# Weight sums with other signs, a part of them added by transfers, in a Strassen-Winograd gate/up projection

## The chip, the cores and the metric

The kernel runs on one core of one Trainium2 chip. The metric is the device time of one launch in microseconds (us). Engines are called PE (TensorE; PEld is its weight load), DVE (VectorE), ACT (ScalarE), POOL (GpSimd) and SP (SyncE, which here issues transfers only).

## The reference

One decoder layer over 512 tokens of width 2048, all in float32: a combined input projection, gated linear attention and dilated attention side by side, an output projection, and a SwiGLU feed-forward part with 5632 hidden columns. The change is in the last line.

```python
h = rms_norm(x, norm1_g)
proj = h @ w_in                     # (512, 2048) @ (2048, 6160)
...                                 # gla_mixer and dilated_mixer
x = x + mix @ w_out                 # (512, 2048) @ (2048, 2048)
h2 = rms_norm(x, norm2_g)
x = x + (silu(h2 @ w_gate) * (h2 @ w_up)) @ w_down      # w_gate, w_up: (2048, 5632)
```

## The kernel before

Every large product is computed in "pairs": 512 tokens by two times 512 weight columns (for the gate pairs 512 columns of w_gate and the same 512 of w_up), as one level of Strassen-Winograd: seven products of quarter blocks instead of eight. The eleven gate pairs (j = 0 to 10) follow the output projection, and six pairs of the down projection follow them.

**Left factors.** The class Operand holds, for each of four row groups of 2 x 256 rows, the four plain or summed quarters of the normalised activations: A11, A12, A22 and S1 to S4. Each one is kept as a high part, rounded to float32r by ACT, and a remainder made by DVE (`split`, L174 and L175). All eleven gate pairs share one operand, `opn`. It is built while the output projection ends and gate pair 0 begins (`operand_jobs`, `early_jobs`, `late_jobs`).

**Right factors.** A pair has four weight quarters per group, a and c from the first matrix, b and d from the second, each a tile of 128 x 1024 float32 (512 KB) from a pool of 12 (`load_quarter`, L222, issued by SP). The products come in the order P1, P5, P6, P3, P7, P2, P4. P1, P3 and P2 use a, d and c as they are. P5 uses b - a, P6 uses d - (b - a), P7 uses d - b and P4 uses c less what P6 used; DVE makes these sums in place (`source`, L256), one of 1024 columns for each of four products and four groups, so 16 in a pair.

**An item** is one product of one group. ACT rounds its weight tile to a high part (`wh`, L331), DVE makes the remainder (`wl`, L335), and PE does eight matmuls with the high part and four with the remainder (L361). Both `wh` and `wl` have two buffers. A pair has 28 items. `stream` runs through the items of all pairs: before the matmuls of item k it writes down the cast of k + 1, the sum of k + 2 and the remainder of k + 1.

**Results.** P1, P5 and P6 leave PSUM as `seeds` (ACT, L282), times the row scale; the later products are added by `close` (DVE, L298). For a gate pair `final_ffn` multiplies silu(gate) with up, transposes on PE (L1109), stores the product to memory (p_d, L1124), and a `sums_job` reads it back (r, L1173) and makes the down projection's left sums on DVE (L1457, L1459, L1462, L1464).

**Order.** Only the first pair has an order written out by hand. After it the framework's scheduler places the instructions of each engine by priority and by when it expects operands, so a sum can be done well before the item that needs it. Each engine then runs its list in order: an instruction that waits holds up all behind it. A load from SP waits until a tile of the pool is free.

POOL issues no transfer. It computes the reciprocal roots of the row norms, the last of them `rs2`, the row scale of the gate pairs (`output_scales`, L1396 to L1401).

Of the kernel before, what the change touches and what calls it, by code (L numbers as in the profile page):

```python
# [18 lines left out]
P = 128  # L19
# [11 lines left out]

PRODUCTS = ("P1", "P5", "P6", "P3", "P7", "P2", "P4")
UPPER_FIRST = ("P1", "P2", "P5", "P6", "P3", "P7", "P4")
SINGLE = {"P1": "a", "P3": "d", "P2": "c"}
SUMS_OF = {"P5": "ba", "P6": "da", "P7": "db", "P4": "ca"}
CLOSES = {"P3": (0, 1), "P7": (1, 1), "P2": (0, 0), "P4": (1, 0)}
# [71 lines left out]
def block_kernel(ctx: ExitStack, tc: tile.TileContext, ins, out):  # L108
# [56 lines left out]
    class Operand:  # L165


        def __init__(self, groups):
            self.groups = groups
            self.t = {}  # L170

        def split(self, name, g, src):
            a = apool.tile([P, 2, 2, 256], F32R, name=nm("A" + name), tag="A")
# [6 lines left out]
        def build(self, g, r11, r21, r12, r22):  # L180

            get = lambda r: r() if callable(r) else r
            tt = nc.vector.tensor_tensor
            r11, r22 = get(r11), get(r22)
            yield
            yield
            self.split("A11", g, r11)
            r21 = get(r21)
            yield
            self.split("A22", g, r22)  # L190
            r12 = get(r12)
            yield
            tt(r22, r21, r22, op=ALU.add)
            self.split("S1", g, r22)
            yield
            tt(r21, r11, r21, op=ALU.subtract)
            tt(r11, r22, r11, op=ALU.subtract)
            self.split("S2", g, r11)
            yield
            tt(r11, r12, r11, op=ALU.subtract)  # L200
            self.split("S4", g, r11)
            yield
            self.split("S3", g, r21)
            yield
            self.split("A12", g, r12)
            yield
# [29 lines left out]
    class Pair:  # L236


        def __init__(self, op, rows, w1, w2, final, step, scale=None, before=None):
            self.op, self.rows, self.w1, self.w2 = op, rows, w1, w2  # L240
            self.final, self.step, self.scale, self.before = final, step, scale, before
            self.q, self.dst, self.held = {}, {}, {}
# [7 lines left out]
        def source(self, prod, g):  # L250

            if prod in SINGLE:
                return self.quarter(SINGLE[prod], g)
            one, two = SUMS_OF[prod]
            src = self.quarter(two, g)
            nc.vector.tensor_tensor(src, self.quarter(one, g), src, op=ALU.subtract)  # L256
            return src

        def accs(self):
            return [acc.tile([P, 512], F32, name=nm("acc"), tag="acc") for _ in range(2)]  # L260
# [10 lines left out]
            if ahead and prod in CLOSES:  # L271
                later(3, lambda: ahead(*CLOSES[prod]))

        def seeds(self, src, half):
            res = []

            def one(m):
                t = cpool.tile([P, 512], F32, name=nm("seed"), tag="C")
                if self.scale is None:
                    nc.scalar.copy(halves(t), unfolded(src[m]))  # L280
                else:
                    nc.scalar.activation(  # L282
                        halves(t), unfolded(src[m]), AF.Copy, scale=self.scale(half, m)
                    )
                res.append(t)

            later(1, lambda: one(0))
            later(2, lambda: one(1))
            return res

        def close(self, seed, src, half, which):
            def one(m):
                if self.scale is None:
                    nc.vector.tensor_tensor(
                        halves(seed[m]), unfolded(src[m]), halves(seed[m]), op=ALU.add
                    )
                else:
                    nc.vector.scalar_tensor_tensor(  # L298
                        halves(seed[m]), unfolded(src[m]), self.scale(half, m), halves(seed[m]),
                        op0=ALU.mult, op1=ALU.add,  # L300
                    )
                if m == 1:
                    self.final(half, which, seed, None)

            later(1, lambda: one(0))
            later(2, lambda: one(1))

        def end(self, prod):
            src = self.dst[prod]
            if prod in ("P1", "P5", "P6"):  # L310
                self.held[prod] = self.seeds(src, int(prod == "P5"))
            elif prod == "P4":
                later(1, lambda: self.final(1, 0, None, src), hold=True)
            else:
                which = {"P3": "P6", "P7": "P5", "P2": "P1"}[prod]
                self.close(self.held[which], src, *CLOSES[prod])

    def stream(pairs):


        items = [(p, prod, g) for p in pairs for prod in PRODUCTS for g in range(p.op.groups)]
        last = len(items) - 1
        sources, high, low = {}, {}, {}

        def total(k):
            p, prod, g = items[k]
            sources[k] = p.source(prod, g)

        def first_part(k):
            high[k] = hpool.tile([P, 2, 512], F32R, name=nm("wh"), tag="wh")  # L330
            nc.scalar.copy(high[k], sources[k])  # L331

        def second_part(k):
            low[k] = hpool.tile([P, 2, 512], F32R, name=nm("wl"), tag="wl")
            nc.vector.tensor_tensor(  # L335
                low[k], sources.pop(k), high[k].bitcast(F32), op=ALU.subtract
            )

        total(0)
        first_part(0)  # L340
        total(1)
        second_part(0)
        for k, (p, prod, g) in enumerate(items):
            if g == 0:
                if prod == "P1" and p.before:
                    p.before()
                p.begin(prod)
            run_soon()
            if k < last:
                first_part(k + 1)  # L350
            if k + 2 <= last:
                total(k + 2)
            if k < last:
                second_part(k + 1)
            a = p.op.t[COMBO[prod], g]
            fresh = prod in ("P1", "P5", "P2")
            for w, terms in ((high.pop(k), (0, 1)), (low.pop(k), (0,))):
                for jj in range(2):
                    for m in range(2):
                        for hl in terms:  # L360
                            nc.tensor.matmul(  # L361
                                p.dst[prod][m], a[:, jj, hl, m * P : (m + 1) * P], folded(w[:, jj, :]),
                                start=fresh and g == 0 and len(terms) == 2 and jj == 0 and hl == 0,
                                stop=g == p.op.groups - 1 and len(terms) == 1 and jj == 1,
                                skip_group_check=not fresh,
                            )
                if len(terms) == 2:
                    p.step()
            if g == p.op.groups - 1:
                p.end(prod)  # L370
# [247 lines left out]
    ss1 = const([P, 4, 4], "ss1")  # L618
    rs1 = const([P, 4], "rs1")
    nrs1 = const([P, 4], "nrs1")  # L620
    row_scale = lambda half, m: rs1[:, 2 * half + m : 2 * half + m + 1]
    raw = {}
    xms = const([P, 4], "xms")
    rs0 = const([P, 4], "rs0")
# [597 lines left out]
    def late_jobs(op, groups, tops, bots, flip):  # L1222

        h0, h1 = (1, 0) if flip else (0, 1)
        tt = nc.vector.tensor_tensor
        sums = {}

        def sum_of(name, g, op1):
            def use(t):
                if name == "S1":  # L1230
                    tt(sums[g], t, sums[g], op=ALU.add)
                elif name == "S2":
                    tt(sums[g], sums[g], t, op=ALU.subtract)
                else:
                    tt(sums[g], t, sums[g], op=ALU.subtract)
                op.split(name, g, sums[g])

            return use
# [152 lines left out]
            yield  # L1391

    ocol = lambda c: w_out[:, c : c + 512]
    def output_scales():
        tmp2 = const([P, 4], "tmp2")
        nc.vector.tensor_tensor(tmp2, ss2[:, :, 2], ss2[:, :, 3], op=ALU.add)  # L1396
        nc.vector.tensor_tensor(tmp2, tmp2, part2, op=ALU.add)
        rsqrt_mean(rs2, tmp2, D)
        nc.gpsimd.tensor_scalar(part2, part2, 2.0 / D, EPS, op0=ALU.mult, op1=ALU.add)
        nc.gpsimd.tensor_tensor(part2, part2, phalf, op=ALU.pow)  # L1400
        nc.gpsimd.tensor_tensor(rs2, rs2, part2, op=ALU.mult)  # L1401

    opn = Operand(4)
    tops = [xn_d[2], xn_d[3], xn_d[6], xn_d[7]]
    bots = [xn_d[0], xn_d[1], xn_d[4], xn_d[5]]
    pair(opm, rows_mix, ocol(0), ocol(512), final_out(0), paced([1] * 28),
# [3 lines left out]

    rows_n = [(512, 0), (768, 256), (1536, 1024), (1792, 1280)]
    p_d = [dram([P, 2, 512], f"p_d{b}") for b in range(22)]
    tok_scale = lambda half, m: rs2[:, 2 * half + m : 2 * half + m + 1]

    def final_ffn(j):
        ups = {}
# [77 lines left out]
    for j in range(11):  # L1494
        c = slice(512 * j, 512 * j + 512)
        pair(
            opn, rows_n, w_gate[:, c], w_up[:, c], final_ffn(j),
            paced(paces.get(j, ())), tok_scale, before=lambda j=j: before_ffn(j),
        )


# [82 lines left out]
```

## Time and profile before

| | |
|---|---|
| median of 3 runs | 1985.19 us (1984.94 to 1986.34) |
| the profiled execution | 1985.91 us, span 1984.0 us |
| mean granted PE clock | 0.994 |
| transfers | 360.45 MB, mean 182 GB/s |
| sums of weights on DVE, L256 | 376 of 128 x 1024, mean 1.22 us each |
| gate pairs 1 to 10 | about 821 to 1568 us of the span |

The time of a run is the whole launch; the span is from the first to the last instruction of the profile. Durations of one instruction include its latency: neighbours in one engine's queue overlap a little, so a row of starts tells the pace better than the mean duration. A line number can be that of a helper, so tile names tell the products apart: wa, wb, wc and wd are the weight quarters, wh and wl the high part and the remainder. In square brackets behind an instruction of the timeline stands how long its engine stood idle before it, and what ended that.

### The profile page before, as it was taken

To read this page: it belongs to the slowest core of one execution; us is meant where nothing else is said; L and a number is where in the kernel's file an instruction comes from. 1 tells how busy PE (TensorE), PEld (TensorE's weight loads), DVE (VectorE), ACT (ScalarE), POOL (GpSimd) and SP (SyncE) were. 2 spreads that over 40 slices of the span, in tenths; PEclk is the share of its full clock that TensorE was granted. 3 is DMA by queue.
4 is the path that set the end of the run, shared out by engine and by line. 5 is a ranking of instruction groups with operands and counts; after the bars stand their busy time and mean duration, and the time that the engine had idled before them with its cause. 6 is when DMAs were issued, how large, how long until landed. Compare 5 with 4: busy or idle time off the path is not lost.

```text
span 1984.0 us, 25786 instructions
## 1 busy us (share of the span) xinstructions
PE 1931.4 (97%) x9226; PEld 1672.0 (84%) x9226; DVE 1653.4 (83%) x1850; ACT 1096.3 (55%) x1600; POOL 62.4 (3%) x81
## 2 busy tenths in 40 slices
PE   7999999999999989999999999999999999999998
PEld 6888888888878777888888888888888888888887
DVE  7997787768689889878878878878879989989887
ACT  7664464566676766545545545545546646546443
POOL 0000231011000000000000000000000000000000
PEclk9999999999999999999999999999999999999999
DMA  8357455454666685553554553554555865865662
GB/s 276 125 169 252 134 173 177 143 155 148 212 212 210 204 276 158 176 170 123 180 166 132 175 166 126 175 164 128 175 165 172 283 208 183 288 202 175 222 212 75
DMA packets 237113, 360.45 MB, mean 182 GB/s; under 512 B 18246, under 2 KB 96783, under 8 KB 236984
## 3 DMA queue, kind: packets, MB, share of 16 engines
q1 hardware_dynamic: 236776, 358.72, 56.9%
q8 instruction: 72, 1.18, 0.3%
q14 instruction: 57, 0.47, 0.1%
q10 hardware_dynamic: 208, 0.08, 0.0%
HBM read 296.59 MB, written 64.51 MB: 182 GB/s over the span
## 4 chain that ended last, share of the span: by engine, by line
PE 83%; DVE 6%; DMA 6%; issue 2%; ACT 1%; SPq 1%; POOL 1%; DVEq 0%; ACTq 0%; POOLq 0%
PE acc L361 75%; PE acc L429 3%; DVE wl L335 2%; PE bank L1109 1%; DVE wa L256 1%; PE bank L1006 1%; PE bank L974 1%; DMA xn_d<-oT 1%; DMA x<-in_x 1%; ACT wh L331 1%; DMA x_d<-q 1%; DVE AS L175 1%; PE bank L999 0%; DMA wc<-in_w_in 0%; PE bank L759 0%
## 5 line engine op out<-in xcount | busy, mean ns | idle before, releaser
L361 PE MATMUL acc<-wh,AS 128*128 128x512 f32 x3008 | 714.0, 380 | 0.0
L361 PEld LDWEIGHTS acc<-wh,AS 128*128 128x128 f32 x3008 | 570.0, 190 | 81.7 <-ACT wh L331 0.4
L331 ACT CAST wh<-wa 128x1024 fp32r<-128x1024 f32 x376 | 393.9, 1049 | 403.7 <-PE acc L361 378.0
L361 PE MATMUL acc<-wh,AA 128*128 128x512 f32 x2256 | 536.0, 380 | 6.6 <-ACT wh L331 6.6
L335 DVE TENSOR_TENSOR wl<-wa,wh 128x1024 fp32r<-128x1024 f32 x376 | 458.4, 1223 | 83.6 <-ACT wh L331 44.3
L361 PEld LDWEIGHTS acc<-wh,AA 128*128 128x128 f32 x2256 | 427.9, 190 | 68.6 <-ACT wh L331 7.8
L361 PE MATMUL acc<-wl,AS 128*128 128x512 f32 x1504 | 395.9, 385 | 7.9 <-DVE wl L335 7.8
L361 PEld LDWEIGHTS acc<-wl,AS 128*128 128x128 f32 x1504 | 279.7, 189 | 60.1 <-DVE wl L335 19.2
L361 PE MATMUL acc<-wl,AA 128*128 128x512 f32 x1128 | 298.8, 387 | 3.6 <-DVE wl L335 3.4
L361 PEld LDWEIGHTS acc<-wl,AA 128*128 128x128 f32 x1128 | 211.0, 190 | 35.9 <-DVE wl L335 6.3
L331 ACT CAST wh<-wb 128x1024 fp32r<-128x1024 f32 x94 | 98.5, 1049 | 119.5 <-PE acc L361 116.2
L331 ACT CAST wh<-wc 128x1024 fp32r<-128x1024 f32 x94 | 98.4, 1047 | 112.3 <-PE acc L361 103.1
L331 ACT CAST wh<-wd 128x1024 fp32r<-128x1024 f32 x94 | 98.6, 1048 | 105.4 <-PE acc L361 101.4
L256 DVE TENSOR_TENSOR wa<-wc,wa 128x1024 f32<-128x1024 f32 x94 | 114.8, 1226 | 43.8 <-DMA wc<-in_w_gate 25.5
L335 DVE TENSOR_TENSOR wl<-wc,wh 128x1024 fp32r<-128x1024 f32 x94 | 115.0, 1224 | 39.9 <-ACT wh L331 38.2
L335 DVE TENSOR_TENSOR wl<-wd,wh 128x1024 fp32r<-128x1024 f32 x94 | 114.9, 1224 | 35.6 <-ACT wh L331 29.1
L335 DVE TENSOR_TENSOR wl<-wb,wh 128x1024 fp32r<-128x1024 f32 x94 | 114.1, 1222 | 4.5 <-ACT wh L331 4.2
L256 DVE TENSOR_TENSOR wb<-wd,wb 128x1024 f32<-128x1024 f32 x94 | 115.0, 1224 | 1.2 <-DMA wd<-in_w_in 0.8
L256 DVE TENSOR_TENSOR wa<-wb,wa 128x1024 f32<-128x1024 f32 x94 | 113.8, 1221 | 0.8
L256 DVE TENSOR_TENSOR wa<-wd,wa 128x1024 f32<-128x1024 f32 x94 | 113.2, 1223 | 0.1
L298 DVE SCALAR_TENSOR_TENSOR seed<-acc,rs,seed 128x512 f32<-128x512 f32 x96 | 70.7, 749 | 24.7 <-PE acc L361 24.7
L282 ACT ACTIVATE seed<-acc,rs 128x512 f32<-128x512 f32 x96 | 60.8, 683 | 1.1 <-PE acc L361 1.0
(283 smaller groups left out, 1370.8 us busy)
## 6 DMA issues: line engine op xcount, KB each, us to landing
wa<-in_w_gate SPq DMA_DIRECT2D x44, 512.0 KB, 3.7
wb<-in_w_up SPq DMA_DIRECT2D x44, 512.0 KB, 4.4
wd<-in_w_up SPq DMA_DIRECT2D x44, 512.0 KB, 4.3
wc<-in_w_gate SPq DMA_DIRECT2D x44, 512.0 KB, 3.6
wc<-in_w_in SPq DMA_DIRECT2D x28, 512.0 KB, 3.7
wa<-in_w_in SPq DMA_DIRECT2D x24, 512.0 KB, 5.0
wb<-in_w_in SPq DMA_DIRECT2D x24, 512.0 KB, 6.6
wd<-in_w_in SPq DMA_DIRECT2D x24, 512.0 KB, 5.9
```

What stands on the lines that cost most here:

```text
L175: nc.vector.tensor_tensor(a[:, :, 1, :], src, a[:, :, 0, :].bitcast(F32), op=ALU.subtract)
L256: nc.vector.tensor_tensor(src, self.quarter(one, g), src, op=ALU.subtract)
L282: nc.scalar.activation(halves(t), unfolded(src[m]), AF.Copy, scale=self.scale(half, m))
L298: nc.vector.scalar_tensor_tensor(halves(seed[m]), unfolded(src[m]), self.scale(half, m), halves(seed[m]), op0=ALU.mult, op1=ALU.add,)
L331: nc.scalar.copy(high[k], sources[k])
L335: nc.vector.tensor_tensor(low[k], sources.pop(k), high[k].bitcast(F32), op=ALU.subtract)
L361: nc.tensor.matmul(p.dst[prod][m], a[:, jj, hl, m * P : (m + 1) * P], folded(w[:, jj, :]), start=fresh and g == 0 and len(terms) == 2 and ...
L429: recent["pe"] = nc.tensor.matmul(dst[prod][m], a[:, jj, hl, m * P : (m + 1) * P], folded(w[:, jj, :]), start=fresh and g == 0 and len(ter ...
L974: nc.tensor.matmul(lp[:, :n], qh[:, b * P : (b + 1) * P], kh[:, :n], start=True, stop=True)
L1006: nc.tensor.matmul(op, vh[:, k, :], lgs[b][:, k * P : (k + 1) * P], start=(k == 0), stop=(k == b))
L1109: nc.tensor.transpose(bk[:, jj, m * P : (m + 1) * P], tiles[m][:, f : f + P], ident)
```

## The change

It has four parts.

1. `Operand` takes a flag `added`, set for `opn` alone. With it S1, S2 and S4 have other signs: S1 is b - a instead of a + b, and S2 and S4 are made by scalar_tensor_tensor as (-1 x one operand) minus the other, where they were plain subtractions.
2. With these left factors the weight sums of the gate pairs are additions: P5 uses a + b, P6 d + (a + b), P7 b + d, P4 c plus what P6 used. P7's sum is now written into d's tile, where it was written into b's.
3. The results of P5, P6, P3 and P7 come out negative, so their row scale is taken from a new table `nrs2` = -rs2, which POOL makes with one more small operation.
4. For the products named in REMOTE (all four in pair 2, P7 in pair 4, P7 and P4 in pair 6) DVE makes no sum. POOL issues a transfer that reads the quarter from memory and adds it onto the tile (`add_remotely`, 28 transfers of 512 KB). It is written down in `stream` five items ahead of the item that uses the sum. A quarter that only remote sums need is not loaded: in pair 2, b.

```diff
+ADDED_OF = {"P5": "ba", "P6": "da", "P7": "bd", "P4": "ca"}
+ALL = ("P5", "P6", "P7", "P4")
+REMOTE = {2: ALL, 4: ('P7',), 6: ('P7', 'P4')}
 SUMS_OF = {"P5": "ba", "P6": "da", "P7": "db", "P4": "ca"}
...
+        def sum(self, name, a, b, out):
+            tt = nc.vector.tensor_tensor
+            if name == "S1":
+                tt(out, b, a, op=ALU.subtract if self.added else ALU.add)
+            elif not self.added:
+                tt(out, a, b, op=ALU.subtract)
+            elif name == "S2":
+                nc.vector.scalar_tensor_tensor(out, a, -1.0, b, op0=ALU.mult, op1=ALU.subtract)
+            else:
+                nc.vector.scalar_tensor_tensor(out, b, -1.0, a, op0=ALU.mult, op1=ALU.subtract)
...
-            tt(r22, r21, r22, op=ALU.add)
+            self.sum("S1", r21, r22, r22)
...
-            one, two = SUMS_OF[prod]
+            one, two = ADDED_OF[prod] if self.op.added else SUMS_OF[prod]
             src = self.quarter(two, g)
+            if prod in self.remote:
+                return src
+            if self.op.added:
+                nc.vector.tensor_tensor(src, self.quarter(one, g), src, op=ALU.add)
+                return src
             nc.vector.tensor_tensor(src, self.quarter(one, g), src, op=ALU.subtract)
             return src
+
+        def add_remotely(self, prod, g):
+            one, two = ADDED_OF[prod]
+            r0 = self.rows[g][0 if one in "ab" else 1]
+            w = self.w1 if one in "ac" else self.w2
+            nc.gpsimd.dma_start(
+                self.quarter(two, g), w[r0 : r0 + 256, :].rearrange("(j p) n -> p j n", p=P),
+                accum_op=ALU.add,
+            )
...
+        def sign(self, half, m, which):
+            return self.scale(half, m, which and self.op.added)
...
             if k < last:
                 second_part(k + 1)
+            if k + 5 <= last:
+                ahead, name, group = items[k + 5]
+                if name in ahead.remote:
+                    ahead.add_remotely(name, group)
             a = p.op.t[COMBO[prod], g]
...
+        nc.gpsimd.tensor_scalar(nrs2, rs2, -1.0, None, op0=ALU.mult)
-    opn = Operand(4)
+    opn = Operand(4, added=True)
...
-    tok_scale = lambda half, m: rs2[:, 2 * half + m : 2 * half + m + 1]
+    def tok_scale(half, m, negative=False):
+        return (nrs2 if negative else rs2)[:, 2 * half + m : 2 * half + m + 1]
...
             opn, rows_n, w_gate[:, c], w_up[:, c], final_ffn(j),
-            paced(paces.get(j, ())), tok_scale, before=lambda j=j: before_ffn(j),
+            paced(paces.get(j, ())), tok_scale, remote=REMOTE.get(j, ()), before=lambda j=j: before_ffn(j),
```

More of the change, by code (lines that the diff above doesn't have):

```diff
@@ L165, in block_kernel, with __init__ @@
     class Operand:
-        def __init__(self, groups):
+        def __init__(self, groups, added=False):
             self.groups = groups
             self.t = {}
+            self.added = added
+        def sum(self, name, a, b, out):
[8 more added lines that the diff above has]
+                nc.vector.scalar_tensor_tensor(out, b, -1.0, a, op0=ALU.mult, op1=ALU.subtract)
         def split(self, name, g, src):
@@ L196, in build @@
             tt(r21, r11, r21, op=ALU.subtract)
-            tt(r11, r22, r11, op=ALU.subtract)
+            self.sum("S2", r22, r11, r11)
             self.split("S2", g, r11)
             yield
-            tt(r11, r12, r11, op=ALU.subtract)
+            self.sum("S4", r12, r11, r11)
             self.split("S4", g, r11)
@@ L236, in block_kernel, with __init__ @@
     class Pair:
-        def __init__(self, op, rows, w1, w2, final, step, scale=None, before=None):
+        def __init__(self, op, rows, w1, w2, final, step, scale=None, before=None, remote=()):
+            self.remote = remote
             self.op, self.rows, self.w1, self.w2 = op, rows, w1, w2
@@ L272, in begin, with seeds @@
                 later(3, lambda: ahead(*CLOSES[prod]))
-        def seeds(self, src, half):
+        def sign(self, half, m, which):
+            return self.scale(half, m, which and self.op.added)
+        def seeds(self, src, half, which):
             res = []
@@ L282, in one @@
                     nc.scalar.activation(
-                        halves(t), unfolded(src[m]), AF.Copy, scale=self.scale(half, m)
+                        halves(t), unfolded(src[m]), AF.Copy, scale=self.sign(half, m, which)
                     )
@@ L298, in one @@
                     nc.vector.scalar_tensor_tensor(
-                        halves(seed[m]), unfolded(src[m]), self.scale(half, m), halves(seed[m]),
+                        halves(seed[m]), unfolded(src[m]), self.sign(half, m, which),
+                        halves(seed[m]),
                         op0=ALU.mult, op1=ALU.add,
@@ L310, in end @@
             if prod in ("P1", "P5", "P6"):
-                self.held[prod] = self.seeds(src, int(prod == "P5"))
+                self.held[prod] = self.seeds(src, int(prod == "P5"), prod != "P1")
             elif prod == "P4":
@@ L620, in block_kernel @@
     nrs1 = const([P, 4], "nrs1")
-    row_scale = lambda half, m: rs1[:, 2 * half + m : 2 * half + m + 1]
+    row_scale = lambda half, m, negative=False: rs1[:, 2 * half + m : 2 * half + m + 1]
     raw = {}
@@ L1224, in late_jobs @@
         h0, h1 = (1, 0) if flip else (0, 1)
-        tt = nc.vector.tensor_tensor
         sums = {}
@@ L1229, in use @@
             def use(t):
[L1230 to L1233, printed above, removed]
+                if name == "S2":
+                    op.sum(name, sums[g], t, sums[g])
                 else:
-                    tt(sums[g], t, sums[g], op=ALU.subtract)
+                    op.sum(name, t, sums[g], sums[g])
                 op.split(name, g, sums[g])
@@ L1393, in block_kernel @@
     ocol = lambda c: w_out[:, c : c + 512]
+    nrs2 = const([P, 4], "nrs2")
     def output_scales():
```

## The prediction

> **What bounds the kernel now.** I read the page's busy shares and its chain first, then a table of the gate pairs, then the order of time around the few stalls. Pairs are counted from 0, as in the table of the change; one "item" is one product of one row group (12 matmuls, one cast, one remainder).
>
> ```profile
> PE 1931.4 (97%) x9226; PEld 1672.0 (84%) x9226; DVE 1653.4 (83%) x1850; ACT 1096.3 (55%) x1600; POOL 62.4 (3%) x81
> PE 83%; DVE 6%; DMA 6%; issue 2%; ACT 1%; SPq 1%; POOL 1%; DVEq 0%; ACTq 0%; POOLq 0%
> ```
> TensorE is busy for 97% of the span and carries 83% of the chain of work that ended last. VectorE, from which the change takes work, has 83% busy and only 6% of the chain.
>
> The table of stretches (length, then busy time and instructions of PE, PEld, DVE, ACT, POOL, clock, DMA share, GB/s) gives gate pairs 0, 1, 2, 3, 4 and 6:
> ```profile
> 748.00:821.00 73.00, 70.61 (x322) 60.45 (x322) 62.48 (x67) 40.44 (x51) 4.95 (x5) 0.98 0.58 173
> 821.00:895.50 74.50, 74.50 (x354) 65.19 (x353) 60.36 (x59) 37.14 (x42) 0.00 (x0) 1.00 0.53 160
> 895.50:972.00 76.50, 74.67 (x354) 65.09 (x354) 60.39 (x59) 37.12 (x42) 0.00 (x0) 1.00 0.52 156
> 972.00:1046.00 74.00, 74.00 (x352) 64.77 (x351) 60.00 (x58) 37.13 (x42) 0.00 (x0) 1.00 0.51 158
> 1046.00:1120.50 74.50, 74.50 (x354) 65.19 (x354) 60.36 (x59) 37.13 (x42) 0.00 (x0) 1.00 0.53 161
> 1195.00:1270.00 75.00, 74.66 (x355) 65.11 (x354) 60.41 (x59) 37.22 (x43) 0.00 (x0) 1.00 0.51 155
> ```
> Pairs 1, 3 and 4 have no PE idle at all. DVE is idle 14 us in each of 74.5. PE loses 1.83 us in pair 2, 0.34 in pair 6 and 2.39 in pair 0. So in the pairs that get adding transfers there are 2.2 us in all that relief of DVE could give back.
>
> The chain in order of time (start, length) gives the pace, and the timeline the stall of pair 2:
> ```profile
> 980.75 62.19 PE acc L361 x288
> 1043.81 10.36 PE acc L361 x48
> ...
> 905.67 0.57 SPq L1124 DMA_DIRECT2D p_d<-PT  x1
> 909.03 2.56 SPq L1173 DMA_DIRECT2D r<-p_d  x4
> 914.65 0.69 DVE L1457 TENSOR_TENSOR r<-r,r 128x512 f32<-128x512 f32 x1 [2.01 <-DMA r<-p_d]
> 916.54 1.13 PE L361 MATMUL acc<-wl,AS 128*128 128x512 f32 x4 [1.83 <-DVE wl L335]
> ```
> 48 matmuls take 10.36 us, so an item takes 2.59. In pair 2 DVE did not run out of time: it stood 2.01 us at the sums of the previous pair's result (L1457), waiting for a transfer, with a remainder (wl) queued behind it.
>
> **The change part by part.** *Sums that leave DVE.* 28 weight sums go: 16 in pair 2, 4 in pair 4, 8 in pair 6. The L256 sums alone, in the stretch of pair 2 (length, DVE busy):
> ```profile
> 895.50:972.00 76.50, 19.42 (x17) 1.00 0.52 156
> ```
> That is 1.14 us each (19.4 over 17): 18 us of DVE in pair 2, 4.6 in pair 4, 9.1 in pair 6. They lie beside PE, which waits for nothing there. A freer DVE doesn't bring the transfer at L1457 forward either, so pair 2's stall stays. Bounds: 0 to -2.2 us; I take 0, since DVE has 14 us to spare.
>
> *The adding transfers.* POOL issues 28, each for the item five ahead. POOL is busy 0.00 us in these stretches, so its wait holds up only later adds. What waits for the add is the cast of the item that uses the sum (L331 on ACT, with the next casts and the seeds of L282 queued behind it); before, it waited for DVE's sum. The target tile is last read by the remainder of the item four earlier, so the add can begin there. How long does it have?
> ```profile
> 894.07 1.23 DVE L335 TENSOR_TENSOR wl<-wa,wh 128x1024 fp32r<-128x1024 f32 x1 [2.02 <-PE acc L361]
> 896.40 1.89 PE L361 MATMUL acc<-wh,AA 128*128 128x512 f32 x8
> 907.64 1.89 PE L361 MATMUL acc<-wh,AS 128*128 128x512 f32 x8
> 927.23 1.05 ACT L331 CAST wh<-wd 128x1024 fp32r<-128x1024 f32 x1 [1.54 <-PE acc L361]
> 928.31 1.22 DVE L335 TENSOR_TENSOR wl<-wd,wh 128x1024 fp32r<-128x1024 f32 x1 [0.94 <-ACT wh L331]
> 930.49 1.89 PE L361 MATMUL acc<-wh,AS 128*128 128x512 f32 x8
> ```
> The cast that starts at 927.23 is for the item that PE begins at 930.49: 3.26 us ahead; it takes 1.05, so it may slip about 2.2 us before PE waits. Pair 2 begins at 896.40 and P5 at 907.64. The first remainder of pair 2 ends at 895.30, so P5's first sum has until 907.64 - 1.1 = 906.5: 11.2 us (10.3 in a stretch without transposes). P5 and P6 follow each other, so eight transfers must be through by the cast of the last, item 11: 896.40 + 0.87 (the transposes: 907.64 - 896.40 less 10.36) + 11 x 2.59 - 1.1 = 924.7. That is 29.4 us for eight, 3.67 each. The four of P7 have from the end of P3's first remainder (929.5) to 930.49 + 7 x 2.59 - 1.1 = 947.5: 18.0 us, 4.5 each.
>
> No add by transfer, and no transfer from POOL, is in the trace. The nearest rows are the plain loads of the same 512 KB (median us to landing) and the queue's total:
> ```profile
> wa<-in_w_gate SPq DMA_DIRECT2D x44, 512.0 KB, 3.7
> wc<-in_w_gate SPq DMA_DIRECT2D x44, 512.0 KB, 3.6
> wa<-in_w_in SPq DMA_DIRECT2D x24, 512.0 KB, 5.0
> wb<-in_w_in SPq DMA_DIRECT2D x24, 512.0 KB, 6.6
> q1 hardware_dynamic: 236776, 358.72, 56.9%
> 895.30:924.70 29.40, 27.57 (x132) 23.77 (x131) 27.33 (x27) 15.01 (x19) 0.00 (x0) 1.00 0.34 117
> ```
> Each alone fits: 3.6 to 6.6 us against 10.3. For the flow, 358.72 MB took 56.9% of 1984 us, 3.15 us per MB, so 1.65 us of all 16 engines per load. In the 29.4 us of P1 to P6 of pair 2 the engines are busy 0.34, 10.0 us. Eight adds at the price of a load bring 13.2: 23.2 of 29.4, it fits. If an add reads its target too and so costs two loads, 26.4 + 10.0 = 36.4: 7.0 us too long. Bounds: 0 to +7.0 in P5/P6; I take 0, from the nearest row, the plain load.
>
> The Trainium skill, Collectives: The Full Stack, section "The bandwidth ceiling: the fold count and why AG ≠ RS ≠ AR", says that an add inside a DMA engine is slowed by its two source reads, not by the adding. By it the sum would be the second one, +7.0; no run shown here has such a transfer. The same skill, DMA: Bandwidth & Descriptors, section "Anatomy of one DMA — SWDGE (gpsimd) path", gives 2.0 us plus bytes over 436 GB/s for a transfer that GpSimd issues, 3.2 us for 512 KB (an estimate by that page); the loads here took 3.6 to 3.7, and by its figure the sum is the first one.
>
> *Transfers that go.* In pair 2 the four loads of b go from SP's queue (every remote sum reads from memory); in pair 6 and pair 4 b is free after P5. Loads are gated by free tiles, and the tiles come free no later than before. 0.
>
> *What the adds collide with.* In pair 2, p_d stores and r loads (rows above: 905.67 to 914.65) now share the engines with the adds of P5. Each 1 us that they slip adds 1 us to the stall at L1457. A freer DVE doesn't help it. Bounds -1.83 (gone) to +1.7 (one more load's engine time in front); I take 0.
>
> *Signs in all eleven pairs.* P7's sum was b = d - b and could be made early (the wb<-wd,wb below lies in P1 of pair 2); now d = b + d must follow P3's remainder of d. Four sums of 1.14 move per pair from the early products to P3/P7. DVE before, with pair 6's stall, which lies 24 us into its pair, in P6:
> ```profile
> 904.61 1.22 DVE L256 TENSOR_TENSOR wb<-wd,wb 128x1024 f32<-128x1024 f32 x1
> 1219.53 1.13 PE L361 MATMUL acc<-wl,AS 128*128 128x512 f32 x4 [0.34 <-DVE wl L335]
> 930.90 1.23 DVE L335 TENSOR_TENSOR wl<-wd,wh 128x1024 fp32r<-128x1024 f32 x1 [1.37 <-ACT wh L331]
> 933.07 1.23 DVE L256 TENSOR_TENSOR wa<-wc,wa 128x1024 f32<-128x1024 f32 x1 [0.94 <-DMA wc<-in_w_gate]
> 934.21 1.22 DVE L335 TENSOR_TENSOR wl<-wd,wh 128x1024 fp32r<-128x1024 f32 x1
> 943.07 1.22 DVE L335 TENSOR_TENSOR wl<-wb,wh 128x1024 fp32r<-128x1024 f32 x1
> ```
> From the remainder at 930.90 to the one at 943.07 are four items in 12.17 us, 3.04 each against PE's 2.59, since P4's sum and its 0.94 of waiting for c stand between them: 1.8 us of the cushion are used, and PE did not wait. With P7's sum in P3, P4's moves to P7 and P2: the same load one product later. c now comes when b is free, one sum (1.14) later than when d was; it lands at 933 and P2 needs it at 930.49 + 8 x 2.59 = 951. So nothing is lost, with +0.5 us per pair as the upper bound; and pair 6's 0.34, among the early products that get emptier, I take as gone: -0.3.
>
> *S2 and S4 of the operand, and the scales.* Eight TENSOR_TENSOR become SCALAR_TENSOR_TENSOR, and POOL has one more small operation.
> ```profile
> L1462 DVE TENSOR_TENSOR r<-r,r 128x512 f32<-128x512 f32 x11 | 7.6, 693 | 0.0
> L805 DVE SCALAR_TENSOR_TENSOR L<-v,L 128x512 f32<-128x512 f32 x4 | 2.8, 689 | 0.0
> 757.46 0.25 POOL L1401 TENSOR_TENSOR rs<-rs,part 128x4 f32<-128x4 f32 x1
> 769.67 1.26 ACT L282 ACTIVATE seed<-acc,rs 128x512 f32<-128x512 f32 x2
> ```
> 693 against 689 ns: 0. The negative scale follows at 757.7 and is wanted at 769.67 by P5's seeds: covered by 12 us.
>
> Sum: 0 (sums) + 0 (adds) + 0 (collision) - 0.3 (signs) + 0 = -0.3 us on the profiled execution, which took 1985.91 us (span 1984.0), 0.72 over the median of 1985.19. On the median: **1984.9 us**, no change.
>
> **The rivals.** *B, the adds are late: slower.* Place: casts of P5 and P6 in pair 2, then P7 and P4. It decides from about 2.4 us of all engines per add ((29.4 - 10.0) / 8; 1.47 times a load). At two loads it gives +7.0, 1992. If one add is on its way at a time with the 5.0 us of the slower loads, 8 x 5.0 - 29.4 = 10.6, and 4 x 5.0 - 18.0 = 2.0 for each of three P7 groups: +16.6, 2002. For it: a read of the target must go somewhere, and P5/P6 have no sum left to do early. Against: engines are two thirds idle there. The Trainium skill's page Collectives: The Full Stack, named above, has this rival's rule.
>
> *C, the DVE order bites: slower.* If P3/P7 lose 0.5 us in the eight or nine pairs that keep the sum there, +4 to +5: 1989.5. Against it: 14 us of slack per pair.
>
> *D, faster.* The stalls of pairs 0, 2 and 6 all go. Pair 0's:
> ```profile
> 749.60 0.69 DVE L1231 TENSOR_TENSOR r<-v,r 128x512 f32<-128x512 f32 x1 [1.75 <-DMA r<-xn_d]
> 755.37 1.13 PE L361 MATMUL acc<-wl,AA 128*128 128x512 f32 x4 [2.14 <-DVE wl L335]
> 750.00:760.00 10.00, 7.86 (x29) 6.26 (x29) 8.69 (x14) 6.88 (x12) 4.95 (x5) 0.83 0.77 240
> ```
> 2.14 us, and a clock of 0.83 in that stretch (1.7 us more of matmul time). With 2.2 from the later pairs: 1985.2 - 6.0 = 1979.2. Against it: pair 0's stall hangs on a transfer of xn_d that the change doesn't touch; only another order of DVE's queue could move it.
>
> *E, the change does nothing:* the forecast's own side.
>
> **How the numbers follow.** A measurement of this kernel can tell about 0.2%, 4.0 us, from no change. Forecast (with E) 0.50, B 0.26, C 0.06, D 0.18. B and C give slower 0.32, D faster 0.18. The forecast's own range is 1982 to 1988. To hold 8 in 10 the range takes in most of D (from 1980.5) and most of B (to 2001).
>
> **What would show it.** Right: PE busy 74.0 to 74.5 in every gate pair from 1 on, DVE near 42 us in pair 2, casts of summed tiles still waiting for "PE acc L361". B would show casts (L331) in P5/P6 of pair 2 waiting for a DMA from in_w_up, and a pair 2 over 78 us. C would show PE waiting for wl in P3 to P2 of pairs 1, 3, 5. D would show the 2.14 at pair 0 gone. The forecast is wrong if an add takes over 2.4 us of all engines, or POOL needs over 3.67 us to issue one.

## The result: 5% slower

The changed kernel takes 2085.19 us (median of 4 runs, 2077.69 to 2088.05) against 1985.18 before (median of 4 beside them): ratio 1.0495, interval 1.0474 to 1.0516. The profiled execution took 2077.69 us, its span is 2075.9 against 1984.0: 91.9 us more to explain. Its busy shares, its chain by engine, and the two queues of transfers by packets, MB and share of 16 engines:

```profile
PE 1957.3 (94%) x9226; PEld 1683.4 (81%) x9226; DVE 1628.9 (78%) x1822; ACT 1095.6 (53%) x1600; POOL 95.4 (5%) x110
PE 61%; issue 12%; DVE 10%; DMA 6%; ACT 2%; POOL 2%; SPq 0%; DVEq 0%; POOLq 0%; ACTq 0%
q1 hardware_dynamic: 235688, 356.62, 53.9%
q0 software_dynamic: 7616, 14.68, 4.6%
```
DVE lost 24.5 us of work, PE fell from 97% to 94% busy, and PE's share of the chain from 83% to 61%. "Issue", time in which an engine waits for nothing that the profile shows, rose from 2% to 12%. The adds are the new queue q0: 28 of 512 KB. Those of P5 and P6 have this row (median us from issue to landing):
```profile
wa<-in_w_up POOLq DMA_DIRECT2D x8, 512.0 KB, 6.1
```

Where the time went is told by the transposes of up and gate (L1109 before, L1150 after), whose first batch ends each pair. The timeline before, then after, for pairs 1 and 2:
```profile
892.07 1.04 PE L1109 MATMUL bank<-mats,seed 128*128 128x128 f32 x8
968.47 1.04 PE L1109 MATMUL bank<-mats,seed 128*128 128x128 f32 x8
```
```profile
894.08 1.04 PE L1150 MATMUL bank<-mats,seed 128*128 128x128 f32 x8
1021.28 1.04 PE L1150 MATMUL bank<-mats,seed 128*128 128x128 f32 x8
```
Pair 2 takes 127.2 us instead of 76.4. In the same way pair 4 takes 85.8 instead of 74.3, and pair 6 103.8 instead of 74.9. The three pairs with adds account for 50.8 + 11.5 + 28.9 = 91.2 of the 91.9 us; elsewhere 4.3 us are lost up to the end of pair 10, and 3.6 gained behind it. Pair 2's timeline, in which a number in brackets is how long the engine stood idle and what ended it, shows how:
```profile
904.11 1.24 POOL L286 DMA_DIRECT2D wa<-in_w_up  x1 [5.06 <-issue]
910.27 1.05 ACT L368 CAST wh<-wa 128x1024 fp32r<-128x1024 f32 x1 [2.74 <-DMA wa<-in_w_up]
910.44 1.20 POOL L286 DMA_DIRECT2D wa<-in_w_up  x1 [5.09 <-issue]
916.46 1.04 ACT L368 CAST wh<-wa 128x1024 fp32r<-128x1024 f32 x1 [3.98 <-DMA wa<-in_w_up]
916.69 1.22 POOL L286 DMA_DIRECT2D wa<-in_w_up  x1 [5.05 <-issue]
917.56 2.73 PE L402 MATMUL acc<-wh,AS 128*128 128x512 f32 x8 [2.57 <-ACT wh L368]
...
948.96 1.21 POOL L286 DMA_DIRECT2D wa<-in_w_gate  x1 [5.13 <-issue]
968.00 1.22 POOL L286 DMA_DIRECT2D wa<-in_w_gate  x1 [5.10 <-issue]
974.62 1.21 POOL L286 DMA_DIRECT2D wd<-in_w_up  x1 [5.39 <-issue]
980.54 1.04 ACT L368 CAST wh<-wd 128x1024 fp32r<-128x1024 f32 x1 [20.99 <-DMA wd<-in_w_up]
981.64 3.78 PE L402 MATMUL acc<-wh,AS 128*128 128x512 f32 x8 [17.13 <-ACT wh L368]
```
Read the starts on POOL. An add issued at 904.11 lands at 910.27, when the cast that waits for it begins, and the next add starts 0.17 us later; so again at 916.46 and 916.69. One add is on its way at a time, 6.3 us from start to start, while PE needs one every 2.59 us. And the order on POOL is not that of the products, nor that in which `stream` writes the adds down: P4's four adds (wa from w_gate, 948.96 to 968.00) stand ahead of P7's (wd, from 974.62), so P7's first cast waits 20.99 us and PE 17.13. The eight matmuls after that take 3.78 us instead of 1.89: from 981.7 to 985.4 PE's granted clock was 0.50. Such stretches lower its mean over the run (0.977 against 0.994).

### The profile page after: what moved, and what is told of

It reads as the page before. It is cut to its first block, busy times and chain, and to the rows that moved or that the text cites. A ratio compares the mean times of both kernels' runs of the same rounds, so it can differ in the third digit from the quotient of the medians.

```text
span 2075.9 us, 25826 instructions
## 1 busy us (share of the span) xinstructions
PE 1957.3 (94%) x9226; PEld 1683.4 (81%) x9226; DVE 1628.9 (78%) x1822; ACT 1095.6 (53%) x1600; POOL 95.4 (5%) x110
## 4 chain that ended last, share of the span: by engine, by line
PE 61%; issue 12%; DVE 10%; DMA 6%; ACT 2%; POOL 2%; SPq 0%; DVEq 0%; POOLq 0%; ACTq 0%
PE acc L402 57%; DVE wl L372 4%; DMA wd<-in_w_up 1%; DVE wa L278 1%; ACT wh L368 1%; PE bank L1150 1%; DVE AS L191 1%; POOL wa L286 1%; DVE wa L276 1%; PE bank L1015 1%; PE bank L1047 1%; DMA xn_d<-oT 1%; DMA T<-p_d 1%; DVE seed L330 0%; PE bank L1040 0%
## 5 line engine op out<-in xcount | busy, mean ns | idle before, releaser
L402 PE MATMUL acc<-wh,AS 128*128 128x512 f32 x3008 | 727.1, 385 | 65.5 <-ACT wh L368 65.5
L402 PE MATMUL acc<-wl,AS 128*128 128x512 f32 x1504 | 403.1, 391 | 10.7 <-DVE wl L372 10.4
L368 ACT CAST wh<-wd 128x1024 fp32r<-128x1024 f32 x138 | 144.7, 1049 | 243.5 <-PE acc L402 156.3
L372 DVE TENSOR_TENSOR wl<-wd,wh 128x1024 fp32r<-128x1024 f32 x138 | 168.1, 1220 | 120.9 <-ACT wh L368 113.3
L368 ACT CAST wh<-wb 128x1024 fp32r<-128x1024 f32 x50 | 52.3, 1047 | 52.9 <-PE acc L402 48.1
L278 DVE TENSOR_TENSOR wa<-wc,wa 128x1024 f32<-128x1024 f32 x50 | 60.7, 1220 | 20.8 <-DMA wc<-in_w_in 14.0
L372 DVE TENSOR_TENSOR wl<-wb,wh 128x1024 fp32r<-128x1024 f32 x50 | 60.8, 1218 | 4.1 <-ACT wh L368 3.9
L278 DVE TENSOR_TENSOR wb<-wd,wb 128x1024 f32<-128x1024 f32 x50 | 60.8, 1217 | 0.7 <-DMA wd<-in_w_in 0.7
L278 DVE TENSOR_TENSOR wa<-wd,wa 128x1024 f32<-128x1024 f32 x50 | 60.0, 1217 | 0.1
L334 DVE SCALAR_TENSOR_TENSOR seed<-acc,rs,seed 128x512 f32<-128x512 f32 x52 | 38.6, 746 | 14.7 <-PE acc L402 14.7
```

The lines of the kernel that those rows point to most:

```text
L334: nc.vector.scalar_tensor_tensor(halves(seed[m]), unfolded(src[m]), self.sign(half, m, which), halves(seed[m]), op0=ALU.mult, op1=ALU.add,)
L372: nc.vector.tensor_tensor(low[k], sources.pop(k), high[k].bitcast(F32), op=ALU.subtract)
L402: nc.tensor.matmul(p.dst[prod][m], a[:, jj, hl, m * P : (m + 1) * P], folded(w[:, jj, :]), start=fresh and g == 0 and len(terms) == 2 and ...
```

## The experiments

Three theories of what spaces the adds were set against each other from the start: T1, the memory for POOL's descriptors (`dynamic_dma_scratch_size=1024`, a number that the kernel had before it had a transfer on POOL) holds one add but not two; T2, POOL always waits for the add before it; T3, the reads of both operands are the limit.

**Signs without adds** (`signs_only`).
```diff
-REMOTE = {2: ALL, 4: ('P7',), 6: ('P7', 'P4')}
+REMOTE = {}
```


> All four parts of the change but the adding transfers (REMOTE is empty, DVE makes every sum). Theory (the adds alone cost the time): as before, 1985 us within 4 us, gate pairs 74.3 us each. Rival (the signs, or the DVE order that follows from them, share in the loss): over 1990 us, with PE idle in P3 to P2 of the pairs that have no add.

1988.77 us against 1984.61, ratio 1.0026 (1.0015 to 1.0038). So the adds make nearly all of the loss, but 4 us, 0.26%, belong to the rest. PE's waits in the gate pairs come to 3.1 us against 2.2; 2.4 us of the difference stand already at 106 us of the span, where the instructions are those of before. These 4 us come up again below.

**Four adds far apart** (`sparse`): pair 2, row group 0 alone.

> Adding transfers in pair 2 alone and there for row group 0 alone: four adds, at least four items (10.4 us) apart. Theory (an add takes 6.0 us and POOL has one on its way at a time; only the succession of adds is too dense): each add lands in time, pair 2 lasts 74 to 77 us, the total is that of the kernel with the signs alone within 3 us. Rival (an add slows what else runs, by doubled reads or by POOL taking something from DVE): pair 2 over 80 us even so.

1995.77 us in one run. No cast waits for an add: 6 us from issue to landing is hidden when adds are 8 us or more apart. But pair 2 takes 78.5 us, 2.1 more than before, since DVE now waits 4.12 us for the transfer r at its sums of the previous pair (2.01 before, 2.69 in `signs_only`) and PE 2.32. The theory held for the adds themselves. The total is 7.0 us over `signs_only`, where at most 3 were expected; 4.0 of them lie behind the last gate pair, where the profiled runs of all the kernels here spread over 5.7 us. One run can't tell more: the ten of `signs_only` reach from 1984.18 to 1995.58.

**Half adds** (`halves`): each add as two of 256 KB.
```diff
+            for j in range(2):
+                nc.gpsimd.dma_start(
+                    self.quarter(two, g)[:, j], rows[:, j], accum_op=ALU.add
+                )
```


> Each add is issued as two transfers of 256 KB. Theory T1 (one add at a time because the descriptor memory of 1024 bytes per partition holds the descriptors of one add of 512 KB but not of two): several halves are on their way together, a whole add then takes the doubled engine time of about 3.4 us instead of 6.3, pair 2 falls from 127 to about 90 us and the total below 2030 us. T2 (POOL always waits for the add before it): each half has the fixed part of its own, 1.2 us of issue and some 3 us of flight, so 8 us or more per sum and a total over 2110 us. T3 (the doubled reads are the limit): spacing stays at 6 us, total unchanged near 2080 us.

2020.75 us; pair 2 takes 93 us. T2 expected over 2110 and T3 no change: both fall, T1 stands.

**More descriptor memory** (`ring1472`, then `ring1088`): 1472 or 1088 bytes per partition instead of 1024, nothing else.

> One number changed: the descriptor memory for POOL's transfers is 1472 bytes per partition instead of 1024 (what SBUF has left). T1 (its size lets one add through at a time): two adds on their way at once, starts 3.4 to 4 us apart instead of 6.3, pair 2 at 90 to 100 us, total about 2020 us. T2 and T3 (POOL waits for the add before it whatever the memory; or doubled reads limit): unchanged, starts 6.3 us apart, about 2080 us.

> Descriptor memory of 1088 bytes per partition, 68 entries of 16 bytes, against 64 before and 92 in the run with 1472. An add of 256 rows is 16 rows per engine; with a read of the source and one of the target for each and one entry for the end it has 33 entries, two adds 66. T1 with two reads per row: 1088 is enough for two adds, as 1472: total about 2015 to 2020 us. If the step came from something else that 1472 gave (more than two adds, or a larger margin): 2050 to 2080 us.

2015.64 and 2008.01 us, with pair 2 at 86.5 and 85.7 us. The start and the end of pair 2 with 1088, then POOL's timeline:
```profile
893.58 1.04 PE L1150 MATMUL bank<-mats,seed 128*128 128x128 f32 x8
979.23 1.04 PE L1150 MATMUL bank<-mats,seed 128*128 128x128 f32 x8
```
```profile
897.14 1.42 POOL L286 DMA_DIRECT2D wa<-in_w_up  x1 [137.33 <-DVE wl L372]
899.86 1.21 POOL L286 DMA_DIRECT2D wa<-in_w_up  x1 [1.31 <-DVE wl L372]
903.43 1.21 POOL L286 DMA_DIRECT2D wa<-in_w_up  x1 [2.36 <-issue]
907.55 1.21 POOL L286 DMA_DIRECT2D wa<-in_w_up  x1 [2.90 <-issue]
910.09 1.21 POOL L286 DMA_DIRECT2D wa<-in_w_up  x1 [1.33 <-issue]
```
The second add starts 2.7 us after the first, and no add of this run landed in under 5.8. 64 more bytes are as good as 448: in pairs 2, 4 and 6 together they give back 70.0 us and 448 bytes 68.5, of the 91.2 lost. So the size of this memory decides whether adds go singly. The count of 33 entries per add, from which 1088 was chosen, put the step between 1024 and 1088 and it came there; the entries themselves stand in no trace, so the count is not shown.

**P4's adds out of the queue** (`no_p4`).
```diff
+REMOTE = {2: ('P5', 'P6', 'P7'), 4: ('P7',), 6: ('P7',)}
```


> P4 is taken out of REMOTE in pairs 2 and 6, all else as in the changed kernel. Theory (POOL's queue has P4's four adds ahead of P7's, so that P7's casts wait for four adds that nobody needs yet): pair 2 falls by four adds of 6.3 us, from 127 to about 102 us, pair 6 from 104 to about 86 like pair 4, total about 2035 us. Rival (the adds that come too late are those of P5 and P6; P4's are hidden): under 8 us gained.

2047.21 us: pair 2 takes 105.9 us instead of 127.2 (21.3 less), pair 6 88.5 instead of 103.8 (15.3 less). The start and the end of pair 2, then POOL's last add of P6 and its first of P7:
```profile
896.56 1.04 PE L1150 MATMUL bank<-mats,seed 128*128 128x128 f32 x8
1002.49 1.04 PE L1150 MATMUL bank<-mats,seed 128*128 128x128 f32 x8
```
```profile
944.93 1.22 POOL L286 DMA_DIRECT2D wa<-in_w_up  x1 [5.26 <-issue]
956.26 1.21 POOL L286 DMA_DIRECT2D wd<-in_w_up  x1 [10.11 <-DVE wl L372]
```
P4's adds, early and wanted by nobody yet, held up the four behind them: 5.3 us for each in pair 2 and 3.8 in pair 6. The full 6.3 don't come back, since P7's first add now waits for P3's remainder instead.

**Plain loads on POOL** (`plain_pool`): no adds, `REMOTE = {2: ('plain',)}`; in pair 2 POOL issues the 16 plain weight loads in SP's place.
```diff
+                self.q[name, g] = load_quarter(
+                    self.rows, name, g, w, nc.gpsimd.dma_start if self.remote else load
+                )
```


> No add at all (DVE makes every sum, signs as in the change); the 16 weight loads of pair 2 are issued by POOL instead of SP, plain, with the descriptor memory of 1024 bytes. If the add reads its target too, a plain load costs 1.6 to 1.7 us of all 16 engines against 3.4 for the add, half the descriptors, and several are on their way at once: starts as close as 2.6 us while each takes 4 to 5 to land. If POOL's path alone is what is slow: starts 5 us or more apart. Total within 5 us of the kernel with the signs alone in both cases, since loads are issued early.

1987.64 us. Its queue of POOL's transfers, the landing of w_gate's a, and its four starts:
```profile
q0 software_dynamic: 2304, 8.39, 1.5%
wa<-in_w_gate POOLq DMA_DIRECT2D x4, 512.0 KB, 4.9
869.78 0.94 POOL L238 DMA_DIRECT2D wa<-in_w_gate  x1 [107.49 <-DVE wd L278]
871.24 0.74 POOL L238 DMA_DIRECT2D wa<-in_w_gate  x1 [0.52 <-DMA wc<-in_w_gate]
874.16 0.72 POOL L238 DMA_DIRECT2D wa<-in_w_gate  x1 [2.18 <-DVE wl L374]
876.55 0.73 POOL L238 DMA_DIRECT2D wa<-in_w_gate  x1 [1.67 <-DVE wl L374]
```
Starts are 1.5 to 2.9 us apart while one takes 4.9 us to land, with the same 1024 bytes: POOL's path doesn't go singly, the add does. The queue is busy 1.5% of 1985.9 us for 16 loads, 1.86 us each and 144 packets; the adds took 4.6% of 2075.9 for 28, 3.41 us each and 272 packets. An add costs the engines 1.8 plain loads of POOL, or 2.1 of SP (1.65 us).

**Three things mended** (`mended`): 1088 bytes, no P4 in REMOTE, and the negative scale in a tile that was there.

> The change with three things mended: descriptor memory of 1088 bytes (two adds at once), no P4 in REMOTE (P7's adds have nothing ahead of them), the negative scale in a tile that is there. What is left is the price of the adds themselves, 20 of them at 3.2 us of all engines and 6 to 7.5 us from issue to landing. In the prediction's sum, eight adds 3.6 to 3.8 us apart take 29 to 30.5 us of the 29.4 that P1 to P6 of pair 2 give: 0 to 1 us late. Theory (the losses are the ring, the order and the shift): 1987 to 1993 us, at most 0.4% over before. Rival (doubled reads alone are enough to lose): over 1996 us.

2003.92 us, ratio 1.0098 (1.0083 to 1.0114): the theory fell, the rival stands. Its stretch of P1 to P6 in pair 2 (length; PE, PEld, DVE, ACT, POOL busy; clock; DMA share; GB/s), and the waits in it:
```profile
895.00:925.00 30.00, 26.82 (x131) 22.95 (x130) 12.38 (x12) 14.02 (x18) 8.68 (x7) 0.98 0.96 212
923.54 0.69 DVE L1500 TENSOR_TENSOR r<-r,r 128x512 f32<-128x512 f32 x1 [7.41 <-DMA r<-p_d]
926.93 2.07 PE L402 MATMUL acc<-wl,AS 128*128 128x512 f32 x4 [5.07 <-DVE wl L372]
```
The DMA engines are busy 0.96 there against 0.34 before. The casts now lose only 0.9 us of PE's time in this pair. The loss has moved to the small transfer that shares those engines: r takes 9.2 us from issue to landing (median of four; 4.8 before, 4.0 in `signs_only`), DVE waits 7.41 us for it, with PE's remainder behind it, and PE 5.07. Pair 2 takes 82.9 us, pairs 4 and 6 lose 4.6 and 4.2 us, and 4.3 us more stand already at the start of pair 1. With the sums of r written down later, as in `later_sums` below, this kernel was not run.

**The 4 us that are not adds** (`signs_noshift`, `before_pad`, `before_pad64`): the signs with the scale kept in the second half of rs2's tile, so that no buffer moves; and the kernel before with an idle tile of 16 bytes per partition (32 with padding), or of 64.
```diff
+    pad = const([P, 4], "pad")          # before_pad64: [P, 16]
     def output_scales():
+        nc.gpsimd.memset(pad, 0.0)
```


> The signs alone again, but with the negative scale kept in the second half of a tile that is there already, so that no buffer moves. In the run with the signs alone 2.4 us of its loss stood at 106 us of the span, where its instructions are those of before. Theory (the loss is the 32 bytes by which all later buffers move, or chance, not the signs): ratio within 0.1% of 1. Rival (the signs' own order of DVE): 0.2 to 0.3% slower, as before.

> The kernel before with one more tile of 128 x 4 at the place where the change has the negative scale (one memset on POOL, nothing reads it). Theory (moved buffers): 0.1 to 0.3% slower, with 1 to 2.5 us of it before 106 us. Rival (the signs): ratio within 0.1% of 1.

> As the run with one tile more, but the tile has 64 bytes per partition instead of 16 (which take 32), so that later buffers move by 64. Theory A (what counts is that buffers lie at a multiple of 64): as before, ratio within 0.1% of 1, and 290 GB/s or more in the first 40 us. Theory B (any move of the buffers costs it): 0.2 to 0.3% slower, under 287 GB/s in the first 40 us, as with the smaller tile.

Ratios: signs without the shift 1.0008 (0.9999 to 1.0018), the idle tile 1.0026 (1.0016 to 1.0036), the tile of 64 bytes 1.0009 (1.0000 to 1.0018). So most of the 0.26% comes from the 32 bytes by which all later buffers move; the idle tile of 64 bytes has the same memset, so it isn't that, and the signs have at most 0.18%. The first 40 us of before, of before_pad and of before_pad64:
```profile
0.00:40.00 40.00, 27.59 (x141) 23.75 (x142) 26.69 (x40) 26.71 (x51) 2.04 (x13) 0.96 0.90 293
```
```profile
0.00:40.00 40.00, 26.97 (x138) 23.41 (x139) 25.70 (x39) 25.70 (x49) 2.15 (x14) 0.96 0.92 284
```
```profile
0.00:40.00 40.00, 27.47 (x138) 23.86 (x139) 25.76 (x39) 25.80 (x49) 2.15 (x14) 0.93 0.89 285
```
The first loads run at 284 GB/s instead of 293, but at 285 with 64 bytes too, where the ratio is better. `signs_noshift` and `later_sums`, where no tile is added, have 292; all other runs have 280 to 286, `mended` too (283), which adds no tile but has more descriptor memory. A part may be the start; the rest of how 32 bytes cost 4 us stays open.

**Pair 2's old stall** (`later_sums`): the kernel before with the sums of L1457 one step later.
```diff
         yield
         yield
+        yield
         tt(s, t, s, op=ALU.add)
```


> The kernel before, in which the sums of a pair's result (L1457 and following) are written down one step later, with no other change. Theory of the prediction (pair 2's 1.83 us are lost at that sum, which waits for a transfer with a remainder queued behind it): the stall of pair 2 goes, pair 2 at 74.3 to 74.6 us instead of 76.4, total 1 to 2 us less. Rival (something else in pair 2 was late): pair 2 unchanged.

The stretch that was pair 2 before, and had 74.67 of 76.50 (pair 2 itself now ends at 968.3):
```profile
895.50:972.00 76.50, 76.50 (x365) 67.09 (x364) 61.85 (x60) 37.94 (x45) 0.00 (x0) 1.00 0.54 163
```
PE has no idle left there, and pair 2 takes 74.3 us. The total is 1983.12 us, ratio 0.9994 (0.9982 to 1.0006): the 2.1 us that the trace shows are too little to tell from the spread of the runs. No version here is clearly faster than the kernel before.

## Why the prediction was wrong

**The step that failed** is the price of an add: "Bounds: 0 to +7.0 in P5/P6; I take 0, from the nearest row, the plain load." An add is not like a plain load in two ways. It costs the engines 3.41 us (3.2 with two on the way), not 1.65; the upper bound had that. And with 1024 bytes of descriptor memory only one is on its way at a time, so they start 6.3 us apart, as soon as the one before has landed; no bound had that, since the one-at-a-time case was held as a rival and priced with a load's 5.0 us.

**The sum with the measured size.** The budgets of pair 2 held. With 6.35 us per add (the median distance of its starts), eight in P5 and P6 are 8 x 6.35 - 29.4 = 21.4 us late. P7's last is the eighth after P4's four: 8 x 6.35 - 18.0 = 32.8. Together 54.2, and pair 2 lost 127.2 - 74.3 = 52.9. Pair 4 lost 11.5 where 4 x 6.3 - 18.0 gives 7.2. The other 4 us lie before its first add:
```profile
1095.55 1.04 PE L1150 MATMUL bank<-mats,seed 128*128 128x128 f32 x8
1135.25 1.21 POOL L286 DMA_DIRECT2D wd<-in_w_up  x1 [139.76 <-DVE wl L372]
```
It starts 39.7 us into the pair, since DVE came late to P3's first remainder, which it waits for. By the prediction's rows that remainder ends 35.6 us into a pair without a stall (929.5 - 892.07 - 1.83).

**The queue.** "so its wait holds up only later adds" was true and was the point: the later adds were P7's, the waiting ones P4's. The prediction gave P4's adds no place in the order. The adds are written down in the order of the products, P7's first; on POOL P4's stood first. They cost 36.6 us in pairs 2 and 6, by `no_p4` (30.5 of the whole span).

**Rival B** was the case that came, at 2002 where 2085 was measured; its condition ("an add takes over 2.4 us of all engines, or POOL needs over 3.67 us to issue one") was met by its first half, with 3.41 us. Its second half was not: issuing took POOL 1.21 us, and what kept the starts 6.3 us apart was the add before. That B named one add at a time was right; it had the time of one too short and P4's place in the queue not at all. The Trainium skill, Collectives: The Full Stack, section "The bandwidth ceiling: the fold count and why AG ≠ RS ≠ AR", agrees with the traces: its two source reads, against 3.41 us per add here and 1.65 to 1.86 per plain load. That rule's own price, +7.0 us for P5/P6, is near the 6.5 us that pair 2 lost in `mended`, where two adds go at once, but by luck: the casts lost 0.9 us there, and the rest lay at the wait for r.

**What held.** DVE's sums were worth nothing to PE: in `sparse`, where four sums leave DVE and every add comes in time, pair 2 didn't shorten (78.5 us against 76.4), and PE's one wait in it stood behind r. The signs, their order on DVE and the other S2 and S4 cost nothing measurable (1.0008, 0.9999 to 1.0018). Pair 2's stall was the transfer at L1457, as read, and it grew by the collision named: DVE waited 2.01 us before, 2.69 in `signs_only`, 4.12 in `sparse`, 7.41 in `mended`. PE's part of it went from 1.83 to 2.32 and 5.07, so the bound of +1.7 held in `sparse` and not in `mended`. In the changed kernel itself DVE waited 0.35 us for r: the late casts hid it. The scale's new tile was priced as an operation only: an idle tile of its size, 16 bytes, cost 0.26%.

## What to carry to other kernels

An engine that is 83% busy but on 6% of the chain is not worth unloading: first show a PE wait that the work causes. Before adding by transfer, see whether the memory set aside for descriptors lets two adds through, and price an add at two loads on all DMA engines plus its whole latency for each one that can't overlap. A queue that goes in order, such as POOL's here, must get its work in order of need; a look-ahead of a fixed number of items in the program didn't ensure that, since the scheduler placed the adds anew.

## What the runs showed of the hardware

- Adding 512 KB onto SBUF took 1.21 us of POOL, 6.0 us from issue to landing with one on its way and 6.2 to 7.9 with two (medians), and 3.2 to 3.4 us of all 16 engines; a plain load on POOL took 0.73 us, 4.1 to 4.9 us and 1.86 us.
- With 1024 bytes per partition of descriptor memory such adds went singly, 6.3 us apart; with 1088 they overlapped, 2.5 to 5.6 us apart in pair 2.
- Moving all later buffers by 32 bytes cost 0.26% (ratio 1.0016 to 1.0036), by 64 bytes 0.09% (1.0000 to 1.0018); how stays open.
- After PE had waited 17.1 us its granted clock was 0.50 for 3.7 us.
